# Five buffers for gates and results in the first branch's projection, and the output projection's first four token tiles taken together, row block by row block

## The chip, the cores and the metric

The kernel runs on one core of one Trainium2 chip. The metric is the device time of one execution in microseconds (us); the time of before is the median of three runs. A profiled execution gives the trace from which all durations here are read. The engines are TensorE (PE; its weight loads are listed as PEld), VectorE (DVE), ScalarE (ACT), GpSimd (POOL) and SyncE (SP), which issues DMA transfers.

## The reference, cut to what matters

One decoder block on 1024 tokens of width 1024: an S5 state-space branch and an attention branch in parallel, merged by gates, then a projection with a residual, then a feed-forward part.

```python
    cond = jax.nn.silu(c)
        mod = (cond @ w_ada[l] + b_ada[l])[:, None, :]
        sh1, sc1, g1, sh2, sc2, g2 = jnp.split(mod, N_ADA, axis=-1)

        h = modulate(rmsnorm(x, norm1_g[l]), sh1, sc1)
        proj = h @ w_in[l]
        u, q, k, v, gate_a, gate_b = jnp.split(proj, IN_SPLITS, axis=-1)
        y_a = s5_branch(u, lam_re[l], lam_im[l], log_dt[l], b_re[l], b_im[l], c_re[l], c_im[l],
                        d_skip[l], w_glu[l], b_glu[l]) @ w_a[l]
        y_b = stick_breaking_attention(q, k, v) @ w_b[l]
        merged = (jax.nn.sigmoid(gate_a) * y_a + jax.nn.sigmoid(gate_b) * y_b) @ w_o[l]
        x = x + g1 * merged

        h = modulate(rmsnorm(x, norm2_g[l]), sh2, sc2)
        ffn = (jax.nn.silu(h @ w_ffn_gate[l]) * (h @ w_ffn_up[l])) @ w_ffn_down[l]
        x = x + g2 * ffn
    return rmsnorm(x, norm_f_g)
```

`s5_branch` ends with a GLU, `y * sigmoid(y @ w_glu + b_glu)`. In attention, scores `z` of a block of 128 queries get a mask, log-sigmoids of them are summed over later keys (`suffix`), and `exp(log_sigmoid(z) + suffix)` weighs the values.

## The kernel before, in words

All products are float32, made from three products of halves: each operand is split in a high and a low part (names ending in `h` and `l`), and `PRODUCTS` lists high x high, high x low and low x high. One 128 x 512 result over a depth of 512 is thus 12 products on PE, over a depth of 1024 24 of them.

The program is written in stages, and a scheduler orders the instructions of each engine from the tiles that they read and write; only attention's products are pinned to their written order. A pool gives each name so many buffers, and a tile waits until its buffer's old content has been used. A pool that opens at addresses (or PSUM banks) of an earlier pool waits for what was done there.

The stages that the change touches, in order:

- `glu` (L1016) ends the S5 branch. Its gate tiles are called `sg`, three buffers in the pool `tp`. Its output is `y2p`.
- `branch_a` (L1045) multiplies `y2p` by `w_a`: for eight channel blocks `m` and two token halves `h`, 16 tiles in all. Per tile: SyncE loads the raw gate from `gD` (L1057), ScalarE takes its sigmoid in place (L1058), PE makes 12 products into one of four banks `ga` (L735, called in `project`), VectorE multiplies bank and gate into a result tile (L1062), and ScalarE's queue stores the result to `nD` (L1063). The gate tile shares name and buffers with `glu` (`sg`, 3), the result tile is `gst` (2 buffers, in the pool `gp`). On SyncE the gate loads stand among the loads of weights and of `aw` (256 KB each, rows of the conditioning, `ada_rest` at L966, summed on VectorE at L977 and L979 in the pool `ap`). The pool `ap` ("ar2") has 14 KB a partition.
- `triangles` (L793) makes attention's lower triangle `tri`, its copy `upto`, and `mask`, on GpSimd and VectorE; `attention` (L917) fills two carried rows with zeros on VectorE (L925). For each unit, `scores` (L850) makes the scores `z` on PE, VectorE adds the mask (L871), GpSimd and ScalarE make the log-sigmoid (L874 to L876), VectorE splits it (L877 to L879); `sums` (L881) adds it up on PE into `acc` with `upto`. Between the pinned products stand fillers in twelves: projections for later heads.
- `branch_b` (L1065) multiplies attention's output by `w_b`, multiplies with the second gate (L1095), adds the tile from `nD`, and splits the sum into the merged blocks `mg`: eight row blocks `k` of each token half, in `pa` and `pb`, with high and low part.
- `attend_out` (L1110) is the output projection. For each column half `c` and each of eight token tiles `t` it makes 24 products over the eight row blocks (L1128) into a bank `wo`, adds the result to `x` (L1131), and for `c == 1` goes on to the norm. The banks `wo` are of the pool `pp`; the pool `tpp` has four banks `tq`, used for transposes for `c == 1`.
- The feed-forward part follows; `operand` (L464) makes its inputs (L473 to L476), and `seven` (L1243) its products (L1247).

Of the kernel before, what the change touches and what calls it, by code (L numbers as in the profile page):

```python
# [9 lines left out]
F32 = mybir.dt.float32  # L10
# [3 lines left out]
ALU = mybir.AluOpType  # L14
# [346 lines left out]
P = 128  # L361
KT = 8
# [19 lines left out]
PRODUCTS = ((0, 0), (0, 1), (1, 0))  # L382
# [45 lines left out]
class Block:  # L428
# [613 lines left out]
    def halves(self, t):  # L1042
        return [[t[:, :, k, 512 * h:512 * h + 512] for k in range(4)] for h in range(2)]

    def branch_a(self, y2p, tp, gp, ap):  # L1045

        nc, i = self.nc, self.i
        src = i["w_a"][0].rearrange("(k p) n -> p k n", p=P)
        for c in range(4):
            w = self.w3(self.weight(src[:, :, 256 * c:256 * c + 256]), 256)  # L1050
            for n in ((8, 9), (10,), (11,), ())[c]:
                self.ada_rest(n, ap, self.sig, 6)
            for m in (2 * c, 2 * c + 1):
                for h in range(2):
                    s = slice(512 * h, 512 * h + 512)
                    gt = tp.tile([P, 512], F32, name="sg", bufs=3)
                    nc.sync.dma_start(out=gt, in_=self.gD[0, P * m:P * m + P, s])  # L1057
                    self.after(nc.scalar.activation(gt, gt, AF.Sigmoid), self.sig)  # L1058
                    ps = self.mm.tile([P, 512], F32, name="mm")
                    self.project(ps, [t[:, :, P * (m % 2):P * (m % 2) + P] for t in w], h, self.halves(y2p), 4)  # L1060
                    o = gp.tile([P, 512], F32, name="gst")
                    nc.vector.tensor_tensor(o, ps, gt, ALU.mult)  # L1062
                    nc.scalar.dma_start(out=self.nD[P * m:P * m + P, s], in_=o)  # L1063

# [36 lines left out]
    def pieces(self, i, a, b, pool, tag, stage=None):  # L1101
# [5 lines left out]
            out.append(self.operand(flat(a[j]), b and flat(b[j]), SIGN_B[i], tiles, self.nc.vector, self.nc.vector, stage))  # L1107
        return lambda p, k: out[k // 2][p][:, 512 * (k % 2):512 * (k % 2) + 512]

    def attend_out(self, mg, g1, const, tp, pp, tpp):  # L1110
        nc, i = self.nc, self.i
        mod, G = self.mod2, self.G2
        x_v = i["x"].rearrange("o (t p) d -> p (o t) d", p=P)
        src = i["w_o"][0].rearrange("(k p) n -> p k n", p=P)
        x1, xhs = [], []
        for c in range(2):
            cs = slice(512 * c, 512 * c + 512)
            gc = g1[:, cs].unsqueeze(1).broadcast_to([P, 2, 512])
            ws = [self.w3(self.weight(src[:, 2 * a:2 * a + 2, cs], scale=gc), 512) for a in range(4)]
            for t in range(KT if c == 0 else 0):  # L1120
                x1.append(self.X.tile([P, 1024], F32, name="x1"))
                nc.sync.dma_start(out=x1[t], in_=x_v[:, t])
            for t in range(KT):
                ps = pp.tile([P, 512], F32, name="wo")
                j = 0
                for k in range(KT):
                    for a, b in PRODUCTS:
                        nc.tensor.matmul(ps, lhsT=mg[t // 4][k][:, a, P * (t % 4):P * (t % 4) + P], rhs=ws[k // 2][b][:, k % 2],  # L1128
                                         start=(j == 0), stop=(j == 23))
                        j += 1  # L1130
                nc.vector.tensor_tensor(x1[t][:, cs], ps, x1[t][:, cs], ALU.add)  # L1131
                if c == 0:
                    continue
                nc.sync.dma_start(out=self.xD[P * t:P * t + P], in_=x1[t])
                if t % 4 == 0:
                    f = [[self.F.tile([P, 2, 512], F32, name=f"f{y}") for _ in range(2)] for y in range(2)]
                xh = self.rp.tile([P, 1024], F32, name="row") if t % 4 == 3 else tp.tile([P, 1024], F32, name="xh")
                xhs.append(xh)
                ss = const.tile([P, 1], F32, name="ss2", bufs=2)
                nc.scalar.activation(xh, x1[t], AF.Square, accum_out=ss)  # L1140
                r = self.rstd(const, ss, 1)
                nc.scalar.mul(xh, x1[t], r)
                if t % 2 == 0:
                    continue
                for k in range(0, KT, 2):
                    q = tpp.tile([P, 512], F32, name="tq").rearrange("p (k t) -> p k t", k=2)
                    s = slice(P * (t % 4 - 1), P * (t % 4 - 1) + 256)
                    for kk in range(2):
                        for tt in range(2):
                            nc.tensor.transpose(q[:, kk, P * tt:P * tt + P], xhs[t - 1 + tt][:, P * (k + kk):P * (k + kk) + P], self.ident)  # L1150
                        o = f[k // 4][k % 4 // 2][:, kk, s]
                        G_, m_ = G[:, k + kk:k + kk + 1], mod[:, k + kk:k + kk + 1]
                        if kk:
                            nc.vector.tensor_scalar(o, q[:, kk], G_, m_, ALU.mult, ALU.add)
                        else:
                            nc.scalar.activation(o, q[:, kk], AF.Identity, bias=m_, scale=G_)
                if t == 3:
                    b11, b21 = f
                    self.B = {2: self.pieces(2, b11, None, self.PA, "pa"), 4: self.pieces(4, b21, b11, self.PA, "pa")}
        b12, b22 = f  # L1160
        self.blocks = b11, b12, b21, b22
# [238 lines left out]
    def run(self):  # L1400
        tc, nc, i = self.tc, self.nc, self.i
        with ExitStack() as es:
# [17 lines left out]
            with ExitStack() as s1:  # L1420
# [5 lines left out]
                gp = gps.enter_context(self.pool("g", GB, side="right"))  # L1426
# [17 lines left out]
                with ExitStack() as s3:  # L1444
                    with self.pool("ta", 2, side="right") as tp, \
                            self.pool("y2", 1, side="right") as y2, self.pool("ga", GAB, PSUM) as ga, self.pool("qx", 6 - GAB, PSUM) as qx:
                        y2p = y2.tile([P, 2, 4, 1024], F32R, name="y2p")
                        self.mm = Turns((ga, "ga"))
                        with self.pool("y", 1, side="right") as yp:
                            self.glu(yp, y2p, tp)  # L1450
                        kp = s3.enter_context(self.pool("k", 2))
                        qp = s3.enter_context(self.pool("q", 2))
                        self.mm = Turns((mm, "mm"), *[(qx, "qx")] * (6 - GAB))
                        qk = [self.qk_proj(0, qp, kp, None)]
                        self.mm = Turns((ga, "ga"))
                        with self.pool("ar2", 1, side="right") as ap:
                            self.branch_a(y2p, tp, gp, ap)
                    self.exp_ln()
                    vp = s3.enter_context(self.pool("v", 2))
                    op = s3.enter_context(self.pool("o", 4))  # L1460
                    with self.pool("tri", 1) as tri, self.pool("work", 1) as work, self.pool("zp", ZPB, PSUM) as self.zp, self.pool("acc", 1, PSUM) as self.accp, \
                            self.pool("mx", MXB, PSUM) as mx:
                        self.avp = mg_
                        self.triangles(tri)
                        self.mm = Turns((mm, "mm"), *[(mx, "mx")] * MXB)
                        qk = [list(qk[0])] + [[None, None] for _ in range(3)]
                        ops = self.attention(qk, qp, kp, vp, op, gp, work)
                        spare = []
                        for pool, n in ((kp, "k"), (qp, "q")):
                            t = pool.tile([P, 2, 512], F32, name=n)  # L1470
                            spare.append((t[:, 0], t[:, 1]))
                    gps.close()
                    self.rp = es.enter_context(self.pool("row", 1, side="right"))
                    g1 = self.rp.tile([P, 1024], F32, name="row")
                    oh = s3.enter_context(self.pool("oh", 6))
                    ops = [self.operand(t, tiles=[(oh.tile if n else vp.tile)([P, 1024], F32R, name="oh" if n else "V") for _ in range(2)])
                           for n, t in enumerate(ops)]
                    tp = s3.enter_context(self.pool("mt", 2))
                    bb = s3.enter_context(self.pool("bb", 6, PSUM))
                    banks = Turns((mm, "mm"), (mg_, "mm"), *[(bb, "bb")] * 6)  # L1480
                    mg = self.branch_b(ops, const, tp, banks, spare, g1)
            with ExitStack() as s4:
# [13 lines left out]
                tp = s4.enter_context(self.pool("ft", 2, side="right"))  # L1496
# [34 lines left out]
```

## Time and profile before

| | us |
|---|---|
| runs | 1520.73, 1520.55, 1516.18 |
| median | 1520.55 |
| the profiled execution's own time | 1517.3 |
| its span in the trace | 1515.5 |
| mean granted TensorE clock | 0.973 |

The span runs from the first to the last instruction of the trace. Busy time of an engine and its share of the span are listed on the page; rows of the timeline give a start, a duration, the engine, the line, the operation, the tile that is written and the tiles that are read, and in brackets the idle time before with what ended it. A busy PE is not PE at its peak. Of the span, 306 to 382 us hold branch_a and what was loaded for it, 380 to 394 us the first units of attention, 739 to 785 us the output projection's first column half, and from 872 us on the feed-forward part's products run.

### The profile page before, as it was taken

What the parts mean: (1) busy time and instruction counts of PE and PEld (TensorE: products, weight loads), DVE (VectorE), ACT (ScalarE), POOL (GpSimd) and SP (SyncE); (2) the same over time, 40 slices, a digit from 0 to 9 for tenths busy, and PEclk for the clock granted to TensorE, in tenths of its full rate; (3) what the DMA queues carried; (4) which work ended last, traced back from release to release, by engine and by line L of the source; (5) the groups of instructions that cost most, each with busy time, mean ns of one, the idle gap of its engine ahead of it and who ended that gap; (6) DMA issues with size and microseconds to landing.
All of it is one profiled execution on the core that took longest, in us unless ns stands there. A gap on an engine that the chain in (4) does not pass through costs nothing.

```text
span 1515.5 us, 18316 instructions
## 1 busy us (share of the span) xinstructions
PE 1422.3 (94%) x6706; PEld 1121.7 (74%) x6706; DVE 1134.3 (75%) x1523; ACT 583.5 (38%) x764; POOL 611.6 (40%) x306
## 2 busy tenths in 40 slices
PE   5898999997999999999799799999999998999995
PEld 3678888786666666658688588888888886888774
DVE  5779985455887988877625886666666769999998
ACT  3321122622474656564317533333333224343323
POOL 1000000102455555424300145444444468788795
PEclk9999999999999999999999899999999999999998
DMA  9555665388111112117523233333333246445312
GB/s 341 139 112 165 160 160 151 123 283 285 42 42 42 36 49 77 49 57 249 178 87 112 84 111 125 105 104 104 105 105 104 87 152 240 147 160 171 106 51 111
DMA packets 180410, 193.55 MB, mean 128 GB/s; under 512 B 28636, under 2 KB 130080, under 8 KB 180320
## 3 DMA queue, kind: packets, MB, share of 16 engines
q1 hardware_dynamic: 171184, 184.86, 38.8%
q10 hardware_dynamic: 8912, 7.48, 1.8%
q8 instruction: 53, 0.87, 0.2%
q14 instruction: 37, 0.30, 0.1%
q0 software_dynamic: 224, 0.05, 0.0%
HBM read 142.40 MB, written 48.76 MB: 126 GB/s over the span
## 4 chain that ended last, share of the span: by engine, by line
PE 40%; DVE 23%; issue 12%; DMA 10%; POOL 9%; ACT 5%; SPq 1%; DVEq 0%; POOLq 0%; ACTq 0%
PE tq L1247 10%; PE wo L1247 8%; PE wo L1128 5%; POOL ws L874 3%; DMA aw<-in_w_ada_dram 3%; PE gu L1247 3%; PE mm L809 2%; PE mm L643 2%; PE mx L809 2%; PE ga L735 1%; PE acc L809 1%; DVE acc L979 1%; POOL pb L1307 1%; PE mx L735 1%; DVE wa L902 1%
## 5 line engine op out<-in xcount | busy, mean ns | idle before, releaser
L874 POOL TENSOR_SCALAR ws<-wa 128x1024 f32<-128x1024 f32 (+1 forms) x40 | 109.3, 2733 | 117.6 <-DVE wa L871 59.0
L473 POOL TENSOR_TENSOR ws<-wb 128x1024 f32<-128x1024 f32 x26 | 64.2, 2471 | 191.1 <-DMA wb<-in_w_ffn_up_dram 88.6
L457 POOL TENSOR_TENSOR wl<-ws,wh 128x1024 fp32r<-128x1024 f32 x12 | 29.1, 2421 | 122.5 <-ACT wh L454 76.5
L294 POOL MEMSET tz<- 128x1024 f32 x4 | 3.8, 954 | 178.0 <-PE mm L643 95.2
L877 DVE TENSOR_TENSOR ws<-wa,ws 128x1024 f32<-128x1024 f32 (+1 forms) x40 | 46.8, 1169 | 35.6 <-ACT ws L876 35.2
L1300 POOL TENSOR_TENSOR pa<-pa,row 128x1024 f32<-128x1024 f32 x22 | 66.2, 3032 | 0.7 <-DMA pa<-in_w_ffn_down_dram 0.7
L875 ACT ACTIVATE ws<-ws 128x1024 f32<-128x1024 f32 (+1 forms) x40 | 38.9, 972 | 69.3 <-POOL ws L874 69.3
L473 POOL TENSOR_TENSOR wgs<-wb 128x1024 f32<-128x1024 f32 x14 | 35.6, 2540 | 73.3 <-DVE wgl L476 31.1
L1238 POOL TENSOR_TENSOR f<-f,f 128x512 f32<-128x512 f32 x30 | 49.0, 1660 | 26.1 <-DVE f L1228 17.6
L879 DVE TENSOR_TENSOR wl<-ws,wh 128x1024 fp32r<-128x1024 f32 (+1 forms) x40 | 55.6, 1390 | 1.1
L979 DVE SCALAR_TENSOR_TENSOR acc<-aw,cond,acc 128x512 f32<-128x512 f32 x56 | 44.0, 786 | 9.3 <-DMA aw<-in_w_ada_dram 8.5
L809 PE MATMUL z<-q,k 64*128 64x512 f32 (+3 forms) x192 | 42.6, 535 | 6.9 <-DVE gst L1062 6.9
L902 DVE TENSOR_TENSOR wa<-wa,acc 128x512 f32<-128x512 f32 (+1 forms) x80 | 46.7, 624 | 2.7 <-PE acc L809 1.8
L454 ACT CAST wh<-ws 128x1024 fp32r<-128x1024 f32 x24 | 25.0, 1048 | 59.7 <-PE wo L1128 34.9
L1227 ACT ACTIVATE f<-f 128x1024 f32<-128x1024 f32 x22 | 23.3, 1061 | 58.7 <-DVE f L1267 31.3
L1329 POOL TENSOR_TENSOR wb<-pa 128x512 f32<-128x512 f32 x23 | 39.6, 1731 | 15.6 <-DVE wxl L1327 5.5
L905 ACT ACTIVATE wa<-wa 128x1024 f32<-128x1024 f32 (+1 forms) x40 | 38.6, 964 | 13.8 <-DVE wa L902 13.8
L1238 POOL TENSOR_TENSOR f<-f 128x512 f32<-128x512 f32 x20 | 42.2, 2128 | 0.0
L1346 PE MATMUL wo<-f,f 128*128 128x512 f32 x132 | 40.6, 389 | 0.0
L476 DVE TENSOR_TENSOR wl<-ws,wh 128x1024 fp32r<-128x1024 f32 x20 | 28.3, 1415 | 15.9 <-ACT wh L475 15.9
L809 PE MATMUL mm<-wa,V 128*64 128x512 f32 (+3 forms) x192 | 39.8, 507 | 0.0
L876 ACT ACTIVATE ws<-ws 128x1024 f32<-128x1024 f32 (+1 forms) x40 | 38.7, 967 | 0.5
(839 smaller groups left out, 4720.5 us busy)
## 6 DMA issues: line engine op xcount, KB each, us to landing
aw<-in_w_ada_dram SPq DMA_DIRECT2D x64, 256.0 KB, 4.5
hD<-f SPq DMA_DIRECT2D x30, 512.0 KB, 2.8
ws<-in_w_in_dram SPq DMA_DIRECT2D x23, 512.0 KB, 5.2
wb<-in_w_ffn_gate_dram SPq DMA_DIRECT2D x44, 256.0 KB, 4.1
wb<-in_w_ffn_up_dram SPq DMA_DIRECT2D x44, 256.0 KB, 4.2
pa<-in_w_ffn_down_dram SPq DMA_DIRECT2D x22, 512.0 KB, 4.7
wb<-hD SPq DMA_DIRECT2D x40, 256.0 KB, 2.8
x<-in_x_dram SPq DMA_DIRECT2D x16, 512.0 KB, 7.4
```

Of the source, the lines that this page charges most:

```text
L473: (add or nc.gpsimd).tensor_tensor(st, a, b, op)
L809: return self.tc.keep_in_program_order(self.nc.tensor.matmul(*args, **kw))
L874: nc.gpsimd.tensor_scalar(st, a, EXACT, None, ALU.min)
L877: nc.vector.tensor_tensor(st, a, st, ALU.max)
L879: nc.vector.tensor_tensor(lt, st, ht.bitcast(F32), ALU.subtract)
L902: nc.vector.tensor_tensor(a[:, x, 0:f], a[:, x, 0:f], r[:, x, 0:f], ALU.subtract)
L979: nc.vector.scalar_tensor_tensor(acc, w[:, j], cj, acc, ALU.mult, ALU.add)
L1128: nc.tensor.matmul(ps, lhsT=mg[t // 4][k][:, a, P * (t % 4):P * (t % 4) + P], rhs=ws[k // 2][b][:, k % 2], start=(j == 0), stop=(j == 23))
L1238: nc.gpsimd.tensor_tensor(o, a, b, op)
L1247: self.nc.tensor.matmul(ps, lhsT=w[x][:, q, k], rhs=self.B[i](y, k), start=(j == 0), stop=(j == 11))
L1300: nc.gpsimd.tensor_tensor(w, w, g2, ALU.mult)
L1346: nc.tensor.matmul(ps, lhsT=o[x][:, P * t:P * t + P], rhs=o[y][:, R], start=(j == 0), stop=(j == 3 * np_ - 1))
```

## The change

It does two things.

First, `branch_a` takes its gate tile as `gt` with five buffers and its result tile as `na` with five buffers, both from its own pool `ap`, instead of `sg` (three, shared with `glu`) and `gst` (two). The pool `ap` grows by ten buffers of 2 KB a partition, to 34 KB, and lies then over addresses in which attention's pools are allotted later.

Second, `attend_out` makes the first four token tiles of the first column half together: it opens four banks of `tpp`, goes through the row blocks `k`, and makes for each of them the three products of all four tiles, through a new function. The additions to `x` come after all 96 products. The other tiles are made as before.

```diff
-    def branch_a(self, y2p, tp, gp, ap):
+    def branch_a(self, y2p, tp, ap):
...
-                    gt = tp.tile([P, 512], F32, name="sg", bufs=3)
+                    gt = ap.tile([P, 512], F32, name="gt", bufs=5)
                     nc.sync.dma_start(out=gt, in_=self.gD[0, P * m:P * m + P, s])
...
-                    o = gp.tile([P, 512], F32, name="gst")
+                    o = ap.tile([P, 512], F32, name="na", bufs=5)
                     nc.vector.tensor_tensor(o, ps, gt, ALU.mult)
                     nc.scalar.dma_start(out=self.nD[P * m:P * m + P, s], in_=o)
...
+    def wo_product(self, ps, t, ks, mg, ws):
+
+        for k in ks:
+            for j, (a, b) in enumerate(PRODUCTS):
+                self.nc.tensor.matmul(ps, lhsT=mg[t // 4][k][:, a, P * (t % 4):P * (t % 4) + P], rhs=ws[k // 2][b][:, k % 2],
+                                      start=k + j == 0, stop=k + j == KT + 1)
...
+            ps = {}
             for t in range(KT):
-                ps = pp.tile([P, 512], F32, name="wo")
-                j = 0
-                for k in range(KT):
-                    for a, b in PRODUCTS:
-                        nc.tensor.matmul(ps, lhsT=mg[t // 4][k][:, a, P * (t % 4):P * (t % 4) + P], rhs=ws[k // 2][b][:, k % 2],
-                                         start=(j == 0), stop=(j == 23))
-                        j += 1
-                nc.vector.tensor_tensor(x1[t][:, cs], ps, x1[t][:, cs], ALU.add)
+                if c or t > 3:
+                    ps[t] = pp.tile([P, 512], F32, name="wo")
+                    self.wo_product(ps[t], t, range(KT), mg, ws)
+                elif t == 0:
+                    for tt in range(4):
+                        ps[tt] = tpp.tile([P, 512], F32, name="tq")
+                    for k in range(KT):
+                        for tt in range(4):
+                            self.wo_product(ps[tt], tt, (k,), mg, ws)
+                nc.vector.tensor_tensor(x1[t][:, cs], ps[t], x1[t][:, cs], ALU.add)
...
-                            self.branch_a(y2p, tp, gp, ap)
+                            self.branch_a(y2p, tp, ap)
```

The change moves instructions on three engines. On GpSimd, between branch_a and attention, the weight pieces of branch_a and of attention's projections (L456, L457), the triangle (L797, L798) and the mask (L802, L805) stand in this order; rows with + stand there now, rows with - stood there before:

```order
+L456 TENSOR_SCALAR wgh<-wgs 128x1024
+L457 TENSOR_TENSOR wgl<-wgs,wgh 128x1024
+L457 TENSOR_TENSOR wl<-ws,wh 128x1024
 L797 MEMSET tri 128x128
 L802 MEMSET mask 128x640
 L798 AFFINE_SELECT tri<-tri 128x128
 L805 AFFINE_SELECT mask<-mask 128x128 x2
-L457 TENSOR_TENSOR wl<-ws,wh 128x1024
-L456 TENSOR_SCALAR wgh<-wgs 128x1024
-L457 TENSOR_TENSOR wgl<-wgs,wgh 128x1024
-L457 TENSOR_TENSOR wl<-ws,wh 128x1024
 L874 TENSOR_SCALAR ws<-wa 128x2x384 x2
```

Triangle and mask moved behind the weight pieces, to the place just ahead of the first unit's L874.

On PE, at the start of the output projection, the last product of branch_b (into `bb`) is followed by the products of the first token tile. Before, with the numbers of the tiles:

```order
L1093 MATMUL bb_6012<-oh_5591,wgl_5849 128x512
L1128 MATMUL wo_6107<-wh_6064,pa_5601 128x512
L1128 MATMUL wo_6107<-wl_6065,pa_5601 128x512
L1128 MATMUL wo_6107<-wh_6064,pa_5601 128x512
L1128 MATMUL wo_6107<-wh_6064,pa_5602 128x512
L1128 MATMUL wo_6107<-wl_6065,pa_5602 128x512
```

and at the same place in the changed kernel:

```order
L1093 MATMUL bb_6012<-oh_5591,wgl_5849 128x512
L1114 MATMUL tq_6107<-wh_6064,pa_5601 128x512
L1114 MATMUL tq_6107<-wl_6065,pa_5601 128x512
L1114 MATMUL tq_6107<-wh_6064,pa_5601 128x512
L1114 MATMUL tq_6108<-wh_6064,pa_5601 128x512
L1114 MATMUL tq_6108<-wl_6065,pa_5601 128x512
L1114 MATMUL tq_6108<-wh_6064,pa_5601 128x512
L1114 MATMUL tq_6109<-wh_6064,pa_5601 128x512
```

The second row block (`pa_5602`) moved from the fourth product to the thirteenth; the next tiles' products with the first row block stand in its place.

On VectorE, at the start of the feed-forward part, sums (L473, into `ft`), the input operands' low parts (L476, into `x1`) and a weight's low part (L476, into `wl`) stand before in this order:

```order
L473 TENSOR_TENSOR ft_7070<-f0_6370,f0_6610 128x1024
L473 TENSOR_TENSOR ft_7076<-f0_6371,f0_6611 128x1024
L476 TENSOR_TENSOR wl_7127<-ws_7128,wh_7126 128x1024
L476 TENSOR_TENSOR x1_7069<-ft_7070,x1_7068 128x1024
L476 TENSOR_TENSOR x1_7075<-ft_7076,x1_7074 128x1024
L473 TENSOR_TENSOR ft_7116<-f1_6372,f1_6612 128x1024
```

and in the changed kernel in this:

```order
L473 TENSOR_TENSOR ft_7070<-f0_6370,f0_6610 128x1024
L473 TENSOR_TENSOR ft_7076<-f0_6371,f0_6611 128x1024
L476 TENSOR_TENSOR x1_7069<-ft_7070,x1_7068 128x1024
L476 TENSOR_TENSOR wl_7127<-ws_7128,wh_7126 128x1024
L473 TENSOR_TENSOR ft_7116<-f1_6372,f1_6612 128x1024
L476 TENSOR_TENSOR x1_7075<-ft_7076,x1_7074 128x1024
```

The first input operand moved ahead of the weight piece, and the second behind one of the sums.

## The prediction

> **What bounds the kernel now.** I read the page's head and slices first, then the rates by stretch, then the waits of the stage that the change touches, then the chain of waits.
>
> ```profile
> span 1515.5 us, 18316 instructions
> PE 1422.3 (94%) x6706; PEld 1121.7 (74%) x6706; DVE 1134.3 (75%) x1523; ACT 583.5 (38%) x764; POOL 611.6 (40%) x306
> ```
>
> TensorE (PE) is busy 94% of the span, so a change that leaves its instructions alone can only win what it idles, 93 us in all, or what it runs at a lower clock. The change touches two places. The first is branch_a with the start of attention behind it; these are the groups of waits from 300 to 400 us (engine, line, what it waited for: us in total, times, longest) that belong to branch_a:
>
> ```profile
> ACT sg L1058 <- DMA sg<-gD: 32.8, 13, 6.5
> DVE gst L1062 <- DMA nD<-gst: 14.3, 8, 4.1
> ...
> PE z L809 <- DVE gst L1062: 6.9, 1, 6.9
> ...
> PE ga L735 <- DVE gst L1062: 2.4, 1, 2.4
> ```
>
> ScalarE waits for gate loads, VectorE for the store that must free one of the two result buffers, and PE pays at two places: 2.4 us inside branch_a and 6.9 us before attention's first score. The chain of waits of the whole run (start us, us, what) says the same of the last tiles:
>
> ```profile
> 367.47 4.92 DMA nD<-gst
> ...
> 373.24 3.73 DMA sg<-gD
> ...
> 377.13 2.25 DMA nD<-gst
> ...
> 381.91 4.17 PE mm L809 x12
> ...
> 882.08 2.72 PE wo L1247 x12
> ```
>
> Stores and gate loads in turn end last, not PE. The last two rows are also one measure of the clock: twelve products of one form took 4.17 us right after the 6.9 us of idle, and twelve of another 2.72 us at full speed. PE's own rows (start us, us) give the stage's plan:
>
> ```profile
> 325.09 0.62 PE L735 MATMUL ga<-y2p,wh 128*128 128x512 f32 x2
> ...
> 325.77 0.62 PE L735 MATMUL ga<-y2p,wh 128*128 128x512 f32 x2
> ...
> 360.61 1.22 PE L735 MATMUL ga<-y2p,wh 128*128 128x512 f32 x2 [2.41 <-DVE gst L1062]
> ...
> 380.26 1.65 PE L809 MATMUL z<-q,k 64*128 64x128 f32 x8 [6.89 <-DVE gst L1062]
> ...
> 386.01 0.92 PE L809 MATMUL z<-q,k 64*128 64x384 f32 x4
> ...
> 389.82 1.13 PE L809 MATMUL z<-q,k 64*128 64x512 f32 x4
> ...
> 393.75 0.33 PE L809 MATMUL acc<-wh,upto 128*128 128x384 f32 x1
> ```
>
> **Part 1, five buffers for gates and results.** *What goes.* Three products start every 0.68 us (325.09 to 325.77). The 16 tiles are 64 such threes, 43.5 us, so without a wait branch_a's products end at 325.1 + 43.5 = 368.6; before, the last began at 373.0. The last eviction follows:
>
> ```profile
> 379.51 0.69 DVE L1062 TENSOR_TENSOR gst<-ga,sg 128x512 f32<-128x512 f32 x1 [1.55 <-DMA nD<-gst]
> ...
> 382.03 0.96 DVE L871 TENSOR_TENSOR wa<-z,mask 128x768 f32<-128x768 f32 x1 [0.50 <-PE z L809]
> ...
> 387.85 0.95 DVE L877 TENSOR_TENSOR ws<-wa,ws 128x768 f32<-128x768 f32 x1
> 388.84 1.06 DVE L878 TENSOR_SCALAR wh<-ws 128x768 fp32r<-128x768 f32 x1
> 389.93 0.96 DVE L879 TENSOR_TENSOR wl<-ws,wh 128x768 fp32r<-128x768 f32 x1
> 391.00 1.23 DVE L871 TENSOR_TENSOR wa<-z,mask 128x1024 f32<-128x1024 f32 x1
> ```
>
> It ends near 369.5 instead of 380.2, and the first score product starts there. If nothing else came in, the gain would be 10.7 us, and 1.4 us more for the slow products behind the idle.
>
> Do five buffers suffice? A buffer is used again after five tiles, 5 x 2.72 = 13.6 us. A store's landing is
>
> ```profile
> DMA to landing us min/median/max: 2.3/4.7/7.0
> ```
>
> so even the longest store leaves 6 us. A gate load waits for the eviction five tiles back, and the longest wait for one was 6.5 us; the same 6 to 7 us are left. With two result buffers the store had 5.4 us for a cycle, which the median nearly fills: that is the old wait.
>
> Do the transfers keep up? The stretches (us; PE, PEld, DVE, ACT, POOL busy; PEclk, DMA share, GB/s):
>
> ```profile
> 310.00:325.00 15.00, 15.00 (x68) 12.43 (x67) 7.67 (x10) 2.06 (x3) 0.00 (x0) 1.00 1.07 355
> 335.00:360.00 25.00, 23.20 (x101) 18.53 (x100) 13.36 (x19) 6.23 (x9) 4.25 (x3) 1.00 0.98 345
> 306.00:382.00 76.00, 66.70 (x286) 53.76 (x285) 42.09 (x58) 17.16 (x24) 10.35 (x9) 0.95 0.88 288
> ```
>
> From 306 to 382 us 76 x 288 = 21.9 MB move. To be done by 372 they need 332 GB/s; 355 and 345 were held for 15 and 25 us. So it fits, with 4 to 7% to spare, and I charge 1 us of slip. The Trainium skill's page "DMA: Bandwidth & Descriptors", Specifications, gives about 358 GB/s to a core from memory; the row of 355 agrees with it as a ceiling, and by that figure alone the bytes need an estimated 61 us and would be done by 367.
>
> *What is added.* The pool that holds the ten new buffers grows from 14 to 34 KB a partition, and now lies over the addresses where attention keeps its triangle, its mask and its carried rows. In the program as built, GpSimd's triangle and VectorE's fill of the rows wait in the changed kernel for all stores, the last among them. Before, triangle and mask were long made:
>
> ```profile
> 306.33 0.20 POOL L797 MEMSET tri<- 128x128 f32 x1 [10.38 <-DVE sg L1040]
> ...
> 307.31 0.59 POOL L805 TENSOR_SCALAR_AFFINE_SELECT mask<-mask 128x128 f32<-128x128 f32 x2
> ...
> 383.13 2.14 POOL L874 TENSOR_SCALAR ws<-wa 128x768 f32<-128x768 f32 x1 [4.97 <-DMA nD<-gst]
> ```
>
> From tri to the mask's end is 306.33 to 307.90, 1.57 us. It now stands behind the last store. That store is issued on ScalarE's queue behind the cast of the last weight for k:
>
> ```profile
> 374.71 1.03 ACT L454 CAST wh<-ws 128x1024 fp32r<-128x1024 f32 x1
> ...
> 385.31 0.85 ACT L875 ACTIVATE ws<-ws 128x768 f32<-128x768 f32 x1 [3.44 <-POOL ws L874]
> 386.19 0.84 ACT L876 ACTIVATE ws<-ws 128x768 f32<-128x768 f32 x1
> ```
>
> That cast waits for branch_a's last products (its buffer is the one they read), so: 368.6 + 1.05 = 369.7 for the cast, 370 for the issue, 2.25 for the landing (the value of the last store in the chain; 2.3 to 7.0 by the line above), 372.2; + 1.57 = 373.8, and VectorE adds the mask to the first scores from there instead of 382.03: 8.2 us sooner. What is queued behind the wait on GpSimd is the mask, then L874 of the first unit; behind the row fills on VectorE the cast of the triangle and L871. The first scores of PE need none of it.
>
> *From there on.* The score bank is single, so the second unit's scores wait until the first is read. PE: scores 369.6 to 371.3, twelve fillers to 374.0, then a wait until 374.8, where L871 has read; 0.92 and twelve fillers (2.72) to 378.5; 1.13 and 2.72 to 382.3, where the first sum (acc) stands. VectorE and its helpers: 373.8 + 0.96 + 2.14 + 0.85 + 0.84 + 0.95 (L877) + 1.06 + 0.96 = 381.6. Both meet at about 382.2 instead of 393.75, 11.5 us sooner. The third unit's mask add, which follows L879 on VectorE, moves from 391.00 to about 381.7, 9.3 us sooner. VectorE is the busier beside PE there, so I take the middle, 10.4, and with the 1 us of slip **9.5 us**.
>
> On the clock, the row of 360.61 shows two products of 1.22 us instead of 0.62 after only 2.41 us of idle, so the 0.8 to 1.5 us of wait before the second scores could cost up to 1.5 us. The Trainium skill, "TensorE: Matmul & The Clock Gate", Part 1, has the clock fall only after an idle window of about 3.4 us; by it this wait would cost no clock, and the 2.41 us of that row speak against its figure. The sum holds either way within its range.
>
> **Part 2, the output projection's first four tiles.** The 96 products stay, in another order; four evictions come after all of them.
>
> ```profile
> 738.97 0.68 DVE L1095 TENSOR_TENSOR gb<-bb,gb 128x512 f32<-128x512 f32 x1
> ```
>
> ```profile
> L1128 PE MATMUL wo<-wh,pa 128*128 128x512 f32 x32 | 11.8, 432 | 8.5 <-DVE gb L1095 8.5
> L1128 PE MATMUL wo<-wb,pa 128*128 128x512 f32 x48 | 11.7, 389 | 0.0
> ```
>
> PE idles 8.5 us before the first product, until that eviction, and 0.0 after it within the stage's rows. Row block by row block would let PE start on the first merged block while later ones are made; but in the program as built the first product waits for the very same eviction as before, since the four banks belong to a pool that opens when branch_b's banks are released. So nothing starts sooner: **0**. Four accumulators in turn cost nothing, as other products that change bank after each three show:
>
> ```profile
> L643 PE MATMUL mm<-pb,wh x32: 388/393/497, 67.5 to 82.3; 128*128 128x512 f32 x32
> ```
>
> 393 ns against 389. The bounds: 96 x 4 ns = 0.4 us of loss below. Above, if PE started when the first blocks are there, at most the 8.5 us and about 1.4 us of the slow clock behind it (32 products at 432 instead of 389 ns). The four evictions, 0.7 us each and now in a row, lie beside the fifth tile's 24 products (5.4 us), which have banks of their own; the cover goes only if VectorE falls behind by more than 2.6 us.
>
> **A side effect, FFN's start.** The order on VectorE swaps two rows there:
>
> ```profile
> 870.06 1.22 DVE L476 TENSOR_TENSOR wl<-ws,wh 128x1024 fp32r<-128x1024 f32 x1
> ...
> 872.46 0.69 PE L1247 MATMUL tq<-x,wxh 128*128 128x512 f32 x1 [1.34 <-DVE x L476]
> ```
>
> The x operand for which PE idles 1.34 us now goes ahead of this row of 1.22 us. What is late next is the weight piece that changed place, wanted after at least twelve products (2.72 us). Gain between 0 and 1.3; I take **1.0**.
>
> **The sum.** 9.5 + 0 + 1.0 = 10.5 us, on a profiled run whose own time is 1517.3 us (span 1515.5 and 1.8 around it): 1506.8. The three runs before have their median at 1520.55, 3.25 us above it, on which scale it is 1510. I take the middle, **1508**. About 0.3%, 4.6 us, is what a measurement of this kernel can tell from no change.
>
> **The rivals.**
> - *Transfers set the stage.* For: over 306 to 382 only 288 GB/s came through, with ScalarE's stores and SyncE's loads each in order, and in the program as built at most eight of both out at once. Against: the two rows above 340. At 320 GB/s the 21.9 MB end at 374.4 instead of 370; the last loads are gates and last weights, so the end shifts by as much: gain 10.5 - 5 = 5 to 6, about 1513. Chance 0.13.
> - *The mask behind a slow store.* If the last store needs 7.0 us instead of 2.25, mask and all that follows are 4.75 later: gain 5.7, about 1513. The store is the last transfer of its stage, with little beside it, hence 0.05.
> - *Slower: the two queues hold each other up.* All gate loads stand on SyncE's queue among 256 KB loads for the conditioning rows, the first two of them no longer ahead of those; a load waiting for a buffer holds all behind it, weights included. It decides where a round of five tiles exceeds 5 x 2.72 = 13.6 us, and it makes the kernel slower when the round exceeds about 18 us: 16 tiles at 3.65 us are 15 us more, which puts the first sum 4.5 us behind 393.75 (1525). The rows give 6.5 + 4.7 us for a round, so 0.06.
> - *The projection starts early after all.* Then 8.5 + 1.4 us more: about 1498. The program as built speaks against it: 0.04.
> - *Nothing happens*, because the old wait only moves whole to the mask: this would need the store at 380, and is in the second rival's tail; it has no chance of its own.
>
> **How the numbers follow.** The forecast has 0.72, with gains of 8 to 13 us: 1505 to 1512 between the two scales. Leaving out at most 2 in 10, the range takes in the first two rivals and the scales' difference: 1502 to 1515. Faster by over 0.3%: the forecast, 0.04 of the early start and some of the rivals at 5 to 6 us, 0.83; within 0.3%: the rest of those rivals, 0.12; slower: 0.05.
>
> **What would show it right or wrong.** Right: no wait of VectorE's L1062 for its store; L735 without a gap; first scores near 370; triangle and mask on GpSimd near 372, and a wait of PE of about 1 us before the second scores; the first wo row, now called tq, still idle about 8.5 us behind L1095. Wrong: GB/s in 325 to 370 that stays under 320, with PE waiting in L735; a first mask add later than 377; or slow products behind the short wait. A span whose gain comes from 740 us instead would refute part 2.

## The result and the profile after

The changed kernel takes 1508.33 us (median of 4 runs, 1507.11 to 1510.83), the kernel before 1520.30 us in the same session (4 runs). The ratio is 0.9926, with a 95% interval from 0.9911 to 0.9941: 11.2 us less (9.0 to 13.5). The forecast was 1508.

The two traces differ by less than the medians: 1515.5 us of span before, 1509.1 after. The profiled execution of before took 1517.3 us, below its median, and that of after 1510.83, above its own. So ratios are used below for what a kernel is worth, and a trace only for where time goes. To take out what differs from run to run ahead of the change, I read **stretches between two products of PE** from each trace.

The waits from 300 to 400 us, of the changed kernel (engine, line, what it waited for: us in total, times, longest):

```profile
ACT gt L1058 <- DMA gt<-gD: 23.5, 7, 8.5
...
DVE row L925 <- DMA nD<-na: 2.9, 1, 2.9
...
PE z L809 <- DVE wa L871: 2.6, 1, 2.6
```

VectorE's wait of L1062 for its store (14.3 us before) is gone, and so are PE's 2.4 us in L735. In their place stands what part 1 brought with it: the fill of the carried rows waits for the last store, and PE waits for the first mask add. PE's rows (start us, us, and in brackets the idle time before):

```profile
369.01 0.39 PE L735 MATMUL ga<-y2p,wl 128*128 128x512 f32 x1
370.59 0.93 PE L809 MATMUL z<-q,k 64*128 64x128 f32 x8 [1.19 <-DVE na L1062]
...
377.03 0.92 PE L809 MATMUL z<-q,k 64*128 64x384 f32 x4 [2.56 <-DVE wa L871]
...
382.43 1.13 PE L809 MATMUL z<-q,k 64*128 64x512 f32 x4
...
386.34 0.33 PE L809 MATMUL acc<-wh,upto 128*128 128x384 f32 x1
```

branch_a's last product starts 4.0 us sooner than before, the first scores 9.7 us sooner, the first sum only 7.4 us sooner. The chain of waits of the changed kernel (start us, us, what; `issue` is time for which the profile shows no wait) shows why:

```profile
370.57 2.79 DMA nD<-na
...
373.58 0.20 POOL tri L797
...
375.01 0.99 POOL mask L805 x2
375.99 0.02 issue
376.02 0.97 DVE wa L871
376.99 0.04 issue
377.03 0.92 PE z L809 x4
377.94 4.56 PE mm L809 x12
```

Store, triangle, mask, mask add, second scores: the chain runs through the triangle and the mask, which were laid over the new buffers. Behind the 2.56 us of idle, the twelve fillers take 4.56 us instead of 2.72.

The rates of the transfers, in the stretches that were shown of before (us; PE, PEld, DVE, ACT, POOL busy; PEclk, DMA share, GB/s):

```profile
310.00:325.00 15.00, 15.00 (x68) 12.43 (x67) 7.58 (x10) 4.67 (x8) 0.00 (x0) 1.00 1.08 358
335.00:360.00 25.00, 25.00 (x112) 20.70 (x111) 16.44 (x22) 6.95 (x10) 4.10 (x3) 1.00 1.02 352
306.00:374.00 68.00, 66.81 (x299) 54.84 (x298) 42.99 (x57) 17.81 (x25) 8.77 (x6) 1.00 0.96 325
```

The same 22 MB (68 x 325) now pass in 68 us instead of 76, and PE is busy for all of the 25 us where it was busy for 23.2.

At the output projection nothing moved ahead of its first product; this is PE's row, and the groups of PE's products there (xcount | busy us, mean ns | idle before):

```profile
730.68 0.79 PE L1114 MATMUL tq<-wh,pa 128*128 128x512 f32 x1 [8.88 <-DVE gb L1095]
```

```profile
L1114 PE MATMUL tq<-wh,pa 128*128 128x512 f32 x32 | 12.2, 462 | 8.9 <-DVE gb L1095 8.9
L1114 PE MATMUL tq<-wb,pa 128*128 128x512 f32 x48 | 11.0, 389 | 0.0
```

8.88 us of idle against 8.51, and behind it products at 462 ns in the mean instead of 432.

### The profile page after: what moved, and what is told of

Its sections match the earlier page's. It is cut to its first block, busy times and chain, and to the rows that moved or that the text cites. A ratio compares the mean times of both kernels' runs of the same rounds, so it can differ in the third digit from the quotient of the medians.

```text
span 1509.1 us, 18300 instructions
## 1 busy us (share of the span) xinstructions
PE 1421.0 (94%) x6706; PEld 1121.5 (74%) x6706; DVE 1137.7 (75%) x1523; ACT 582.8 (39%) x764; POOL 610.9 (40%) x306
## 4 chain that ended last, share of the span: by engine, by line
PE 51%; DVE 20%; issue 10%; POOL 9%; DMA 5%; ACT 4%; SPq 1%; DVEq 0%; POOLq 0%; ACTq 0%
PE tq L1257 10%; PE wo L1257 8%; PE ga L735 4%; PE wo L1114 4%; PE mm L735 3%; PE mm L809 3%; PE gu L1257 3%; PE mx L809 3%; POOL ws L874 3%; PE mm L643 2%; PE mx L735 2%; PE tq L1114 2%; PE acc L809 1%; POOL pb L1317 1%; PE z L809 1%
## 5 line engine op out<-in xcount | busy, mean ns | idle before, releaser
L874 POOL TENSOR_SCALAR ws<-wa 128x1024 f32<-128x1024 f32 (+1 forms) x40 | 108.5, 2712 | 112.9 <-DVE wa L871 59.2
L473 POOL TENSOR_TENSOR ws<-wb 128x1024 f32<-128x1024 f32 x26 | 64.2, 2471 | 193.8 <-DVE f L1164 90.9
L457 POOL TENSOR_TENSOR wl<-ws,wh 128x1024 fp32r<-128x1024 f32 x12 | 28.9, 2410 | 127.0 <-ACT wh L454 127.0
L473 POOL TENSOR_TENSOR wgs<-wb 128x1024 f32<-128x1024 f32 x14 | 34.6, 2473 | 72.3 <-DVE wgl L476 30.9
L900 ACT CAST row<-acc 1x1024 fp32r<-1x1024 f32 (+2 forms) x32 | 27.0, 842 | 31.2 <-PE acc L809 31.0
```

The costliest lines, as they stand in the source:

```text
L473: (add or nc.gpsimd).tensor_tensor(st, a, b, op)
L874: nc.gpsimd.tensor_scalar(st, a, EXACT, None, ALU.min)
```

## The experiments

Each kernel was timed beside the kernel before on one chip, 4 to 12 runs of it, in four sessions (the changed kernel; `p1_alone` to `gt_only`; `tri_early`, `tri_na_early`, `tq_early` and `all_early`; the rest), so rows of different sessions compare through their ratios only. Shifts in us are the ratio's distance from 1, times 1520.

| kernel | ratio (95%) | us against before | first `ga` to first `acc`, us in the trace |
|---|---|---|---|
| before | 1 | 0 | 68.7 |
| the changed kernel | 0.9926 (0.9911 to 0.9941) | -11.2 | 60.6 |
| the changed kernel, second session | 0.9929 (0.9910 to 0.9948) | -10.8 | 58.9 |
| p1_alone | 0.9937 (0.9917 to 0.9957) | -9.6 | 58.9 |
| p2_alone | 1.0011 (0.9995 to 1.0027) | +1.7 | 69.4 |
| na_only | 0.9955 (0.9938 to 0.9973) | -6.8 | 64.0 |
| gt_only | 0.9979 (0.9965 to 0.9994) | -3.2 | 65.5 |
| bufs3 | 0.9946 (0.9934 to 0.9958) | -8.2 | 61.4 |
| tri_early | 0.9907 (0.9887 to 0.9927) | -14.1 | 58.5 |
| tri_na_early | 0.9903 (0.9884 to 0.9923) | -14.7 | 56.3 |
| tq_early | 0.9858 (0.9838 to 0.9879) | -21.6 | 59.7 |
| tq_tilewise | 0.9882 (0.9866 to 0.9897) | -17.9 | 58.9 |
| all_early | 0.9840 (0.9820 to 0.9860) | -24.3 | 56.3 |

The last column is the distance between the starts of branch_a's first product and of attention's first sum, 325.09 and 393.75 in the trace of before.

**Which part carries the gain.** `p1_alone` is the kernel before with these lines, `p2_alone` the changed kernel without them:

```diff
-                    gt = tp.tile([P, 512], F32, name="sg", bufs=3)
+                    gt = ap.tile([P, 512], F32, name="gt", bufs=5)
-                    o = gp.tile([P, 512], F32, name="gst")
+                    o = ap.tile([P, 512], F32, name="na", bufs=5)
```

> Part 1 alone (five buffers each for gates and results), the output projection as before. My theory: the whole gain comes from here, so 9 to 12 us less than before (ratio 0.992 to 0.994), first sum of attention (acc) at about 386 us in the trace instead of 393.75, GpSimd's triangle behind the last store at about 373 us, and PE's 8.5 us of idle before the first wo product unchanged. Rival, part 2 carries a third of the gain: 6 to 8 us less than before.

> Part 2 alone (first four token tiles of the output projection together), branch_a as before. My theory: nothing that can be measured, -1.5 to +1.5 us against before; the first product of the projection still idles 8 to 9 us behind L1095. Rival, part 2 carries a third of the gain: 3 to 4 us less than before, with a gain that begins behind 740 us in the trace.

Part 1 alone gives 9.6 us (6.5 to 12.6), part 2 alone nothing (-0.8 to +4.1 us). The rival that splits the gain is out: it needed 3 to 4 us less from `p2_alone`. In the trace of `p1_alone` the first sum stands at 382.34 us, sooner than expected because branch_a began 1.7 us earlier and no slow products followed; the projection's first product idles 8.3 us, as before. In the trace of `p2_alone`, it waits for the same eviction, though for less than the 8 to 9 us expected:

```profile
740.44 0.80 PE L1114 MATMUL tq<-wh,pa 128*128 128x512 f32 x1 [6.58 <-DVE gb L1095]
```

**Gates or results.** `na_only` takes only the second pair of lines above, `gt_only` only the first.

> Only the result tile gets five buffers (na), the gate tile stays sg with three. My theory: the wait of VectorE for the store is what bound branch_a, so most of the gain is here: 7 to 10 us less than before, L735 with less than 1 us of idle; the three gate buffers (cycle 3 x 2.72 = 8.2 us) just do. Rival, the gate loads bound it: less than 4 us.

> Only the gate tile gets five buffers (gt), the result tile stays gst with two. My theory: the stores in two buffers still bound branch_a, -2 to +2 us against before, with VectorE's waits for nD<-gst at 10 us or more in all. Rival, the gate loads bound it: 6 us or more less than before.

Most of the gain comes with the results, as expected, though 6.8 us are just under the 7 to 10 forecast. The gates bring 3.2 us alone, more than I had allowed; the two add up to 10.0, close to the 9.6 of both. The waits of VectorE show the two limits in turn, first in `na_only`, then in `gt_only`:

```profile
DVE na L1062 <- ACT sg L1058: 11.9, 5, 2.8
```

```profile
DVE gst L1062 <- DMA nD<-gst: 14.7, 9, 3.1
```

With results free, VectorE waits 11.9 us for gates; with gates free, 14.7 us for stores, as before (14.3). Either limit alone still costs most of the stage's idle: up to the first scores PE idles 5.8 us in `na_only` (0.80 and 5.00) and 6.1 in `gt_only` (3.40 and 2.72), against 9.3 before (2.41 and 6.89).

**Three buffers instead of five.** `bufs3` is the changed kernel with `bufs=3` at both tiles.

> The changed kernel with three buffers for gates and three for results instead of five. My theory: a round of three tiles is 3 x 2.72 = 8.2 us; a gate needs the eviction, a load of 4 to 8.5 us and the sigmoid, so the gates wait now and then as in na_only, which had three gate buffers too: 6 to 9 us less than before, 2 to 4 us more than the changed kernel. Rival, three are enough: within 1 us of the changed kernel.

8.2 us less than before against 10.8 for five in the same session. The medians differ by 3.3 us (1513.40 and 1510.10), the intervals overlap, so it is likely but not shown by the times that five buffers are better than three. The trace has the mechanism that was expected: VectorE waits for the sigmoid of a gate, and PE ends with 3.7 us of idle before the first scores.

```profile
DVE na L1062 <- ACT gt L1058: 7.9, 7, 2.4
...
PE z L809 <- DVE na L1062: 3.7, 1, 3.7
```

**The cost of the overlap.** `tri_early` makes triangle, mask and carried rows in a pool on the right side that is opened before branch_a (the triangle in a free `gst` buffer); `tri_na_early` moreover gives the results a pool of their own, under attention's values.

```diff
+                tri = gps.enter_context(self.pool("tri", 1, side="right"))
...
+                        self.triangles(tri, gp)
+                        self.carried(tri)
-                        with self.pool("ar2", 1, side="right") as ap:
-                            self.branch_a(y2p, tp, ap)
+                        with self.pool("ar2", 1, side="right") as ap, self.pool("na", 1) as np_:
+                            self.branch_a(y2p, tp, ap, np_)
...
-                        self.triangles(tri)
```

> The changed kernel, with triangle, mask and carried rows made before branch_a in addresses of their own (the results stay in branch_a's pool, over which attention's wa lies). My theory: the mask behind the last store is what holds the first mask add at 376.0, so without it wa0 starts when the last store has landed, near 373.5: 2 to 4.5 us less than the changed kernel (the 2.56 us of PE idle before the second scores shrinks to under 1 us and its slow products, 1.8 us, go): 13 to 16 us less than before. Rival, VectorE is the bound there and the gain is eaten within attention's first units: within 1 us of the changed kernel.

> As tri_early, and the result tiles in a pool of their own that lies under attention's values, so that the first mask add waits for no store at all. My theory: wa0 at about 371.6, first sum at about 382, 3.5 to 5 us less than the changed kernel, 14 to 17 us less than before. Rival: within 1 us of the changed kernel.

In the trace of `tri_na_early` the idle before the second scores is gone (PE rows):

```profile
368.58 0.93 PE L817 MATMUL z<-q,k 64*128 64x128 f32 x8 [1.12 <-DVE na L1064]
372.38 0.92 PE L817 MATMUL z<-q,k 64*128 64x384 f32 x4
376.19 1.13 PE L817 MATMUL z<-q,k 64*128 64x512 f32 x4
380.12 0.33 PE L817 MATMUL acc<-wh,upto 128*128 128x384 f32 x1
...
393.81 0.47 PE L817 MATMUL acc<-wh,upto 128*128 128x512 f32 x1 [1.19 <-DVE row L912]
```

The fillers behind the second scores fit into 3.81 us with them, at full speed. So the added wait did cost what it was priced at in the stage: 60.6 - 56.3 = 4.3 us in this pair of traces, 2.6 against the trace of `p1_alone`, where the idle was as long but no slow products followed. A later sum waits 1.19 us for VectorE's L912; the changed kernel has no such wait in its first trace and one of 1.61 us in its second, so this is not a price of the edit. By the ratios, 3.5 us come off the 11.2 of the changed kernel, but the intervals (0.9884 to 0.9923, 0.9911 to 0.9941) overlap, and `tri_early` lies between. In `tri_early` the mask add still waits for the last store (4.5 us on VectorE), and 1.58 us of PE's idle remain where under 1 us was expected. The wait is shown; its worth in the whole kernel is not separated from zero.

**What part 2 lacks.** `tq_early` opens the four banks before branch_b, which keeps four of eight:

```diff
-                    bb = s3.enter_context(self.pool("bb", 6, PSUM))
-                    banks = Turns((mm, "mm"), (mg_, "mm"), *[(bb, "bb")] * 6)
+                    tpp = es.enter_context(tc.tile_pool(name="tq", bufs=TQB, space=PSUM, side="right"))
+                    bb = s3.enter_context(self.pool("bb", 2, PSUM))
+                    banks = Turns((mm, "mm"), (mg_, "mm"), *[(bb, "bb")] * 2)
```

> The changed kernel, with the four tq banks opened ahead of branch_b, which then has four banks instead of eight. My theory: part 2 gave nothing only because its first product waits for branch_b's last eviction through the banks; with free banks PE starts on the first row blocks right behind branch_b's products, waits up to 3 us for weights, and the projection's first four tiles end 6 to 9 us sooner: 16 to 20 us less than before. Rival, the weights or VectorE's evictions are the next bound, or four banks are too few for branch_b: within 2 us of the changed kernel.

21.6 us less than before, about 10.4 less than the changed kernel, more than I had expected. PE goes from branch_b into the projection without a gap (the first two rows below), does not wait for weights either, and the products keep their full speed. Four banks are almost enough for branch_b: PE waits once, 1.29 us before L994, for an eviction (L1095), which it does in none of the kernels with eight.

```profile
723.50 0.39 PE L1093 MATMUL bb<-oh,wgl 128*128 128x512 f32 x1
723.73 0.39 PE L1114 MATMUL tq<-wh,pa 128*128 128x512 f32 x1
...
745.49 0.39 PE L1114 MATMUL wo<-wh,pb 128*128 128x512 f32 x1
```

The same two ends in the changed kernel:

```profile
721.41 0.39 PE L1093 MATMUL bb<-oh,wgl 128*128 128x512 f32 x1
...
755.44 0.39 PE L1114 MATMUL wo<-wh,pb 128*128 128x512 f32 x1
```

From branch_b's last product to the fifth tile's first there are 745.49 - 723.50 = 22.0 us, against 755.44 - 721.41 = 34.0 in the changed kernel and 763.07 - 730.80 = 32.3 before. `tq_tilewise` keeps the free banks and undoes the order by row blocks:

```diff
-                elif t == 0:
-                    for tt in range(4):
-                        ps[tt] = tpp.tile([P, 512], F32, name="tq")
-                    for k in range(KT):
-                        for tt in range(4):
-                            self.wo_product(ps[tt], tt, (k,), mg, ws)
+                else:
+                    ps[t] = tpp.tile([P, 512], F32, name="tq")
+                    self.wo_product(ps[t], t, range(KT), mg, ws)
```

> As tq_early (the four tq banks opened ahead of branch_b), but the first four token tiles one after the other, all row blocks of a tile before the next tile, as before the change. My theory: the free banks alone let PE start, but the first tile needs the last row blocks after 21 products (4.8 us), so PE waits again until the eighth row block and the fourth weight piece are there at about 733 us; 4 to 6 us slower than tq_early, that is 15 to 17 us less than before. Rival, the order by row blocks is worth nothing and the banks are all: within 1.5 us of tq_early, 20 to 23 us less than before.

17.9 us less than before, between the two theories. The banks alone are worth about 7 us, the order by row blocks about 3.7 more. The intervals of the two kernels overlap, and they ran in different sessions; the stretch in the traces says the same as the medians (22.0 us become 750.40 - 724.61 = 25.8). PE does wait again, but for a weight piece and only for 1.92 us, with slow products behind it:

```profile
729.37 0.39 PE L1114 MATMUL tq<-wl,pa 128*128 128x512 f32 x1
731.68 2.86 PE L1114 MATMUL tq<-wb,pa 128*128 128x512 f32 x6 [1.92 <-DVE wb L457]
```

In the order that the scheduler made, 21 products run ahead of that wait, eight of them already of the second tile; my expectation of a fixed order tile by tile had not allowed for those.

**Both together.** `all_early` joins `tri_na_early` and `tq_early`.

> tri_na_early and tq_early together. My theory: both gains add, 10 to 13 us less than the changed kernel, 20 to 25 us less than before. Rival: one of them alone.

24.3 us less than before, 1496.88 us in the median of five runs, the fastest version here. Most is from `tq_early` (1500.27 beside it); the two gains add to 13.9 (3.5 and 10.4) by the single runs, and 13.1 were measured. Against `tq_early` alone, the earlier triangle and mask take off 2.7 us, but the intervals overlap here too.

**The changed kernel again**, beside `bufs3` and `tq_tilewise`:

> The changed kernel itself, unedited, beside the two others on one chip: 10 to 12 us less than before.

10.8 us less than before. Its runs reach from 1504.83 to 1515.46, which is the spread that all small differences here have to be read against.

## Why the prediction was right, step by step

- **What bounds the stage** (stores and gate loads in turn, not PE, not the rate of the transfers): right. Both limits are there, and each is seen alone in `na_only` and `gt_only`. The rate rose to 352 and 358 GB/s without PE waiting, so the rival in which transfers set the stage did not come, and neither did the 1 us of slip; 306 to 374 us ran at 325 GB/s, close to the 332 that had been worked out as needed. The 358 GB/s that the prediction takes for a ceiling are none here: `p1_alone` moved 371 GB/s from 335 to 360 us. Nor do five buffers always leave 6 us: in `p1_alone` VectorE waits once for a store, 2.0 us, without PE waiting.
- **branch_a in 43.5 us**: right. Its last product starts 43.3 us after its first (325.72 to 369.01). The first scores were put at 369.6 and came at 370.59, with a start of branch_a 0.6 us later.
- **The added wait behind the last store**: right in kind, too small in size. The mask was put at 373.8 and ended at 375.99. The store was issued 0.6 us later than worked out and landed in 2.79 us instead of 2.25, a value taken from the last store but two of the kernel before, whose own last store took 3.6; triangle and mask took 2.41 us instead of 1.57, with VectorE's fill now beside them (the last section has the rows); and GpSimd's last weight piece, whose 2.39 us I had not put into the chain, ended 0.3 us after the store had landed:

```profile
371.25 2.39 POOL L457 TENSOR_TENSOR wl<-ws,wh 128x1024 fp32r<-128x1024 f32 x1 [9.33 <-ACT wh L454]
373.58 0.20 POOL L797 MEMSET tri<- 128x128 f32 x1
```

- **PE's wait before the second scores**: put at 0.8 to 1.5 us, it was 2.56, and the slow products behind it that were given up to 1.5 us took 4.56 - 2.72 = 1.8. So the first sum came at 386.34 instead of 382.2. The stretch from branch_a to it shrank by 8.0 us in this trace and by 9.8 in the second one of the same kernel. The 9.5 us forecast for part 1 stand against 9.6 measured for it alone.
- **Part 2 at 0**: right (+1.7, -0.8 to +4.1), and for the reason given: the banks, 8.88 us of idle as against 8.51. The rival's price for an early start, 9.9 us, was near as well: 10.4 when the banks were free, of which some 7 came without the new order.
- **FFN's start, 1.0 us**: this step failed. The row did move, and the second wait fell from 1.34 to 0.76 us, but the wait for the first x operand was longer, first before, then in the changed kernel:

```profile
870.13 0.99 PE L1247 MATMUL tq<-x,wxh 128*128 128x512 f32 x2 [2.48 <-ACT x L475]
```

```profile
862.70 0.50 PE L1257 MATMUL tq<-x,wxh 128*128 128x512 f32 x1 [3.63 <-ACT x L475]
863.96 0.80 PE L1257 MATMUL tq<-x,wxh 128*128 128x512 f32 x1 [0.76 <-DVE x L476]
```

  3.63 + 0.76 = 4.39 us of idle stand against 2.48 + 1.34 = 3.82 before. `p1_alone` has the new waits (2.82 and 0.76) and `p2_alone` the old ones (2.91 and 1.34), so in these two the swap came with part 1, not with part 2. The first wait lies between 1.98 and 4.05 us in the traces of all kernels, in the new order as in the old; what sets it was not looked into. The 0.6 us that the swap takes off the second wait are lost in that.
- **The sum**: 10.5 us, against 11.2 and 10.8 measured. Its first term was right as a whole (10.4 less 1 us of slip is 9.4, not 9.5), but partly by luck: the middle that it takes between PE's 11.5 and VectorE's 9.3 us and the slip that did not come make up for last steps that were late. The third term was not there. That 1508 met the median to 0.3 us is luck too: it is the middle between two scales 3 us apart.

## What to carry to other kernels

A ring of buffers has to outlast the whole round of its tile, landing included: here two results made a cycle of 5.4 us against a median landing of 4.7, and freeing only one of two such rings brought 7 or 3 us of 10. Before a pool is enlarged, ask which later pool its addresses belong to: what had been made long ahead can fall behind the last store. A new order on an engine is worth nothing while its accumulators are released by what it was to run beside: alone it brought nothing, banks of their own brought about 7 us, and the order with them about 10.

## What the runs showed of the hardware

Waits of nearly one length met different clocks. Behind 2.56 us of idle the changed kernel's fillers took 4.56 us; in `p1_alone`, 2.44 us of idle at the same place were followed by products at full speed, and in `tq_early` 3.25 us were:

```profile
374.58 0.92 PE L809 MATMUL z<-q,k 64*128 64x384 f32 x4 [2.44 <-DVE wa L871]
375.43 0.74 PE L809 MATMUL mm<-pa,wh 128*128 128x512 f32 x2
```

```profile
377.52 0.92 PE L809 MATMUL z<-q,k 64*128 64x384 f32 x4 [3.25 <-DVE wa L871]
378.37 0.73 PE L809 MATMUL mm<-pa,wh 128*128 128x512 f32 x2
```

A wait of about 2.5 us thus cost either nothing or 1.8 us more. The granted clock agrees and shows where the waits differ. In these traces its stretches of half clock last 3.41 us or a multiple of it, on a grid of such steps; two steps of the changed kernel and two of `p1_alone` (us; PE, PEld, DVE, ACT, POOL busy; PEclk, DMA share, GB/s):

```profile
375.01:378.42 3.41, 1.39 (x6) 0.79 (x7) 2.19 (x4) 0.00 (x0) 2.33 (x4) 1.00 0.51 143
378.42:381.83 3.41, 3.41 (x9) 2.63 (x8) 1.37 (x2) 1.69 (x2) 2.87 (x2) 0.50 0.00 0
```

```profile
370.58:374.00 3.42, 1.56 (x7) 0.94 (x6) 2.12 (x4) 0.00 (x0) 2.87 (x6) 1.00 0.47 138
374.00:377.41 3.41, 2.83 (x13) 1.92 (x14) 1.48 (x2) 0.62 (x1) 2.80 (x2) 1.00 0.05 15
```

The changed kernel's wait left 1.39 us of work in one step, and the next step ran at half the clock. The longer wait of `tq_early` fell across two steps with 1.63 and 1.96 us of work, and the clock stayed; the 1.92 us of `tq_tilewise` before L1114 fell into one step with 1.49, and it dropped. For these waits it was thus the place that counted, not the length alone. Nor is idle time all that counts: in the kernel before, the clock dropped at 708.77 us though PE shows as busy throughout the step ahead; for the first 2.1 us of it, PE made products of one column (L1005, 128x1). The Trainium skill, "TensorE: Matmul & The Clock Gate", Part 1, calls the window in which activity is watched free-running, which fits; the idle of about 3.4 us that it names as the limit was not needed here: 2.41 us in the kernel before and 2.56 us in the changed one were followed by slow products already.

Two small operations side by side hindered each other. GpSimd's two memsets took 0.20 and 0.63 us in the kernel before, and 0.74 and 1.18 us in `p1_alone`, beside VectorE's fill of 1.39 us:

```profile
370.93 0.74 POOL L797 MEMSET tri<- 128x128 f32 x1
371.61 1.18 POOL L802 MEMSET mask<- 128x640 f32 x1
```

In the changed kernel's trace the memsets ran at 0.20 and 0.63 us, and VectorE's fill took 2.12 us, against 1.29 in the kernel before. That these two engines share ports to their memory, as the Trainium skill says in "SBUF — State Buffer", Terms, fits both rows; no run here isolates it.
